# HGRN output norm of a hybrid decoder layer: sums in full fp32 on four groups of 32 partitions, roots on 256 columns, repeated by way of memory

## The chip, the cores and the metric

The kernel runs on one core of one Trainium2 chip. Five engines work beside each other, each through its own queue, in order: TensorE (PE, matrix products and transposes through the array), VectorE (DVE), ScalarE (ACT), GpSimd (POOL), and SyncE (SP), whose queue issues nearly all transfers (DMA) between memory (DRAM) and the on-chip memory of 128 partitions (SBUF). PE writes its products into PSUM, a small memory of banks of 128 x 512 fp32 values. The metric is the device time of one execution in microseconds (us).

## The reference

One inference step of one decoder layer for a prompt of 1024 tokens and eight single new tokens, 1032 columns together. A combined input projection feeds two mixers: a gated linear recurrence (HGRN2, 8 heads of width 128) and a Mamba-2 mixer. Both end in a gated RMS norm, an output projection and a residual; a gated MLP with a convolution follows. The change touches the norm of the HGRN outputs:

```python
def rmsnorm(x, w):
    xf = x.astype(jnp.float32)
    y = xf * lax.rsqrt(jnp.mean(xf * xf, axis=-1, keepdims=True) + EPS)
    return (y * w.astype(jnp.float32)).astype(x.dtype)
...
o_a, S_h_new = hgrn2_mix(heads(q), heads(k), heads(i_r.astype(f32)), heads(log_f), S_h.astype(f32))
o_a = rmsnorm(o_a, w['hgrn_norm_w']) * jax.nn.silu(heads(g_r).astype(f32))
...
x = x + jnp.concatenate([o_a, y], axis=-1) @ w['w_out']
```

For each head and each token the mean runs over the 128 values of the head's output.

## The kernel before

All activations lie transposed: features on the 128 partitions, tokens along the columns. The mean over a head's 128 features is therefore a sum over partitions, and PE takes it: a product with a matrix of ones leaves the same sum in every output partition.

**The driving stream.** The weight products are cut into jobs (one job for each 128 columns of the input projection and for each pair of 128-column blocks of the output projection). A projection job (`in_job`, L290) has three column chunks of 344 tokens; each weight and each activation is split into a high and a low fp32r part, so that one chunk takes 24 products. `drive` (L266) advances the jobs by so many single products for each weight that a second stream yields, and that stream puts its own instructions in between. `tick` (L233) counts the single products, and `after(n, work)` (L229) lets `work` emit its instructions n products later. PE's queue has exactly this order (the block at L1114); on the other engines a planner orders the instructions. `fetch` (L172) is a transfer on SP's queue that is placed behind the last weight load in the queue (`last_w`).

**A head.** `head` (L830) is the second stream for one head: it transposes v, multiplies the decays into k and q in seven levels (`scale`, L867: DVE), forms the products near the diagonal into 32 partitions at a time (`near`, L882), handles the eight single tokens ("od", L939 to L942: eight products into four groups of 32 partitions), builds the states, then the outputs in two halves of 512 tokens. While head h runs, the jobs of head h + 1 drive; while the last head (7) runs, the first output jobs do, from o8.0 on, with the Mamba-2 rows of the mixed activations read and split on the way (`mix_load`, L1021: "ml" and "mh").

**The norm of a head** (L977 to L1008). For each half, ACT squares the outputs twice from PSUM, once rounded to fp32r (`hl`, name "sqhl") and once in fp32 (`sq`); DVE multiplies weight and gate into the output (`oh`, a half of tile `sg`) and forms the low part of the square by a subtraction. One yield of 3.5 later PE sums high and low part with the fp32r ones (`ones_r`, L529) into a bank "hms" of its own per half, 512 columns each. `rstd_of` (L648) makes the reciprocal root: one table function on ACT, then three DVE instructions that refine it. POOL multiplies it into the output (L1003), and SP stores the finished head (`mix_d`, L1008). The eight single tokens have a small norm of their own ("od", "dms"), which the change leaves as it is.

The weight of a projection job is loaded (`ws`, L189), cast by ACT (`wh`, L190), and its low part is taken by DVE (`wl`, L192). Names from the next head's start that the prediction uses: `vd` (L843, L844: a small tile stored to memory and fetched back repeated on all partitions as `vb`, L852), `v<-q,f` (L902), `tt` (L879), `xtd` and `odr` (L798, L944), `xs` (L784, L794).

Of the kernel before, what the change touches and what calls it, by code (L numbers as in the profile page):

```python
# [8 lines left out]
F32 = mybir.dt.float32  # L9
F32R = mybir.dt.float32r  # L10
U8 = mybir.dt.uint8
AF = mybir.ActivationFunctionType
ALU = mybir.AluOpType
# [3 lines left out]
P = 128  # L17
# [3 lines left out]
NT = T + ND  # L21
# [3 lines left out]
H = 8  # L25
# [25 lines left out]
def hybrid_layer(  # L51
# [9 lines left out]
    V, A, G, PE, SP = nc.vector, nc.scalar, nc.gpsimd, nc.tensor, nc.sync  # L61
# [5 lines left out]
    dram = ctx.enter_context(tc.tile_pool(name="dscr", bufs=1, space=DRAM))  # L67
# [3 lines left out]
    def nm(s):  # L71
        cnt[0] += 1
        return f"{s}_{cnt[0]}"
# [4 lines left out]
    const = part.enter_context(tc.tile_pool(name="const", bufs=1, side="right"))  # L78
# [3 lines left out]
    def tl(tag, name, dt=F32):  # L82
        w, n = TAGS[tag]
        return (work if tag in ("hT", "big", "e", "g") else tmp).tile([P, w], dt, tag=tag, bufs=n, name=nm(name))

    def half(name):
        return tl("s", name)[:, :512]

    def bank(s, tag="mx"):
        return psmx.tile([P, 512], F32, tag=tag, bufs=NBANK[tag], name=nm(s))  # L90

    def mm(out, lhsT, rhs, start=True, stop=True):
        PE.matmul(out, lhsT, rhs, start=start, stop=stop)  # L93
# [55 lines left out]
    def col(name, i=0):  # L149
        c = vlay[name] + i  # L150
        return vcol[:, c:c + 1]
# [20 lines left out]
    def fetch(dst, src):  # L172

        with tc.issue_after(last_w[0].ins):
            SP.dma_start(dst, src)
# [53 lines left out]
    def after(n, work):  # L229

        later.append([n, work])
# [109 lines left out]
    mix_d = dram.tile([16, P, NT], F32, name="mix_d")  # L341
# [60 lines left out]
    ones = keep.tile([P, P], F32, name="ones")  # L402
# [24 lines left out]
    for c, cs in enumerate(chunks):  # L427
        ps = psmm.tile([P, 512], F32, tag="mm", name=nm("dt"))
# [96 lines left out]
    for g in range(4):  # L525
        rows = slice(32 * g, 32 * g + 32)
        V.tensor_copy(mlow[rows], lowf[rows, :, rows])
        V.tensor_copy(eyec[rows], ident[rows, rows])
    ones_r = const.tile([P, P], F32R, name="ones_r")  # L529
    V.tensor_copy(ones_r, ones)  # L530

    def ssd_front(g, c, parts):
        tsl = slice(c * P, (c + 1) * P)
# [114 lines left out]
    def rstd_of(dst, tmp, ps, n):  # L648

        A.activation(dst, ps, AF.Abs_reciprocal_sqrt, bias=epsc, scale=1.0 / n)  # L650
        V.scalar_tensor_tensor(tmp, ps, n * EPS, dst, op0=ALU.add, op1=ALU.mult)
        V.scalar_tensor_tensor(tmp, tmp, -0.5 / n, dst, op0=ALU.mult, op1=ALU.mult)
        V.scalar_tensor_tensor(dst, tmp, 1.5, dst, op0=ALU.add, op1=ALU.mult)
# [76 lines left out]
    def once(work):  # L730
        def run():
# [19 lines left out]
    G.affine_select(eye8, eye8, pattern=[[1, ND], [-1, ND]], compare_op=ALU.is_equal, fill=0.0, base=0,  # L751
                    channel_multiplier=0)
    vd_d = dram.tile([H, ND, P], F32, name="vd_d")

    am = const.tile([P, NC, P], F32, name="am")
    G.memset(am, 0.0)
# [73 lines left out]
    def head(h, t):  # L830
        f, k, q, v, sg = (t[n] for n in ("f", "k", "q", "v", "sg"))
# [5 lines left out]
        for hf in range(2):  # L837
            ps = bank("vtp")
# [22 lines left out]
        hb = [slice(0, 512), slice(512, T)]  # L861
        kt, SS, sq = ([None, None] for _ in range(3))
# [57 lines left out]
        ps = bank("a3")  # L920
# [9 lines left out]
        ps, p6 = bank("a5"), bank("a6")  # L930
# [9 lines left out]
        for b in range(ND):  # L940
            g = b % 4
# [5 lines left out]
        for hf in range(2):  # L947
            kt[hf] = half("kt")
            ps = bank("ktp")
# [5 lines left out]
        for hf in range(2):  # L955
            SS[hf] = half("SS")
            ps = bank("kv")
# [16 lines left out]
        yield 3.2  # L974


        hls = []  # L977
        for hf in range(2):
            oh = sg[:, hb[hf]]
            ps = bank("o")  # L980
            for i in range(4):
                n = hf * 4 + i
                Sb, c = before[n], slice(n * P, (n + 1) * P)
                mm(ps[:, blk[i]], vt[hf][:, blk[i]], am[:, n, :], stop=Sb is None)
                if Sb is not None:
                    mm(ps[:, blk[i]], Sb, q[:, c], start=False)
            sq[hf] = half("sq")
            hl = tl("e", "sqhl", F32R)
            A.activation(hl[:, :512], ps, AF.Square)
            A.activation(sq[hf], ps, AF.Square)  # L990
            V.scalar_tensor_tensor(oh, ps, col("hn"), oh, op0=ALU.mult, op1=ALU.mult)
            V.tensor_tensor(hl[:, 512:1024], sq[hf], hl[:, :512].bitcast(F32), op=ALU.subtract)
            hls.append((oh, hl))
        dps = bank("dms", "nx")
        mm(dps[:, :ND], ones, od[:, 1, :])
        rstd_of(od[:, 1, :], od[:, 2, :], dps[:, :ND], P)
        yield 3.5
        for hf, (oh, hl) in enumerate(hls):
            ps = bank("hms")
            mm(ps, ones_r, hl[:, :512], stop=False)  # L1000
            mm(ps, ones_r, hl[:, 512:1024], start=False)
            rstd_of(sq[hf], half("nt"), ps, P)
            G.tensor_tensor(oh, oh, sq[hf], op=ALU.mult)  # L1003

        oh = sg[:, T:NT]
        V.scalar_tensor_tensor(oh, od[:, 0, :], col("hn"), oh, op0=ALU.mult, op1=ALU.mult)
        V.tensor_tensor(oh, oh, od[:, 1, :], op=ALU.mult)
        SP.dma_start(mix_d[h], sg[:, :NT])  # L1008


    def split(src, hi, lo):
# [102 lines left out]
    with tc.manual_schedule(engines={mybir.EngineType.PE}):  # L1114
        finish("x3")
        drive(ssd(0), 45.5, "x7")
        drive(ssd(1), 45.5, "v0")
        finish("z7")
        for h in range(H):
            drive(head(h, heads[h]), 32.0 if h else 35.0, f"sg{h + 1}" if h < H - 1 else "o12.2")  # L1120
        finish("o12.6")
        for r0 in (0, 4):
            mixes[r0] = mix_load(r0)
# [238 lines left out]
    with tc.manual_schedule(engines={mybir.EngineType.PE}):  # L1362
# [43 lines left out]
        def down(w, kt, msl, acts, c):  # L1406
            q = quarters[c]
            ps = psmm.tile([P, 512], F32, tag="mm", name=nm("dn"))[:, :q.stop - q.start]
            for k in range(kt):
                hi, lo = acts[k]  # L1410
                wh, wl = w(k)
                mm(ps, wh[:, msl], hi[:, q], start=(k == 0), stop=False)
                mm(ps, wh[:, msl], lo[:, q], start=False, stop=False)
                mm(ps, wl[:, msl], hi[:, q], start=False, stop=(k == kt - 1))
                tick()
            return ps

        acts = [act_load(k) for k in range(RND)]
        for r0 in range(0, FT - RND, RND):
# [3 lines left out]
            for m in range(0, KT, 2):  # L1423
                wh, wl = wload(w_down[0, rows, m * P:(m + 2) * P], nk, 2 * P)
                for i in range(2):
# [3 lines left out]
                    for c, cs in enumerate(quarters):  # L1429
                        ps = down(lambda k: (wh[:, k, :], wl[:, k, :]), nk, slice(i * P, (i + 1) * P), acts, c)  # L1430
# [14 lines left out]
    for c in (3, 0, 1, 2):  # L1445
        cs = quarters[c]
        for m in range(KT):
            ps = down(lambda k: wd[k], nk, slice(m * P, (m + 1) * P), acts, c)
# [52 lines left out]
```

## Time and profile before

| | us |
|---|---|
| median of 3 runs | 1769.57 (1768.42 to 1771.63) |
| the profiled execution | 1770.87 |
| its span in the trace | 1769.2 |
| TensorE clock granted, mean | 0.993 of full speed |
| norm of the first head: its first sum on PE | 445.2 |
| norm of the last head: its first sum on PE | 884.0 |
| last read of a head's output from memory (`ml`) issued | 954.0 |

A row of grouped instructions reads: line, engine, operation, written tile <- read tiles, shape, count | busy time in us, mean duration of one in ns | idle time of the engine just before. A row of the timeline begins with its start and its duration in us; "x4" means that four such instructions in a row are merged; the bracket names idle time before and what ended it. "SPq" is SP's queue of transfers: the time is that of the issue. A row of waits reads: engine, tile, line <- what ended the wait: us in total, times, longest. A row of windows gives from:to in us, its length, the busy time (and instructions) of PE, PE's weight loads, DVE, ACT and POOL, the granted TensorE clock, the share of the DMA engines, and GB/s. An fp32 product leaves two records on PE, an fp32r product one.

### The profile page before, as it was taken

What the parts mean: (1) busy time and instruction counts of PE and PEld (TensorE: products, weight loads), DVE (VectorE), ACT (ScalarE), POOL (GpSimd) and SP (SyncE); (2) the same over time, 40 slices, a digit from 0 to 9 for tenths busy, and PEclk for the clock granted to TensorE, in tenths of its full rate; (3) what the DMA queues carried; (4) which work ended last, traced back from release to release, by engine and by line L of the source; (5) the groups of instructions that cost most, each with busy time, mean ns of one, the idle gap of its engine ahead of it and who ended that gap; (6) DMA issues with size and microseconds to landing.
All of it is one profiled execution on the core that took longest, in us unless ns stands there. A gap on an engine that the chain in (4) does not pass through costs nothing. (4 is left out here: it accounts for less than half of the span.)

```text
span 1769.2 us, 38520 instructions
## 1 busy us (share of the span) xinstructions
PE 1717.5 (97%) x16079; PEld 1669.4 (94%) x16079; DVE 1123.7 (64%) x2013; ACT 824.7 (47%) x1474; POOL 503.6 (28%) x501
## 2 busy tenths in 40 slices
PE   7999899999999999999899989999999999999998
PEld 6998799989999999999799989999999999999997
DVE  6668967575554565467646677776666667445545
ACT  7577698454545454454423364343333444111114
POOL 2103332120110110112230355766666664000002
PEclk9999999999999999999999999999999999999999
DMA  5355744543221222234336742222222225422212
GB/s 165 66 148 151 188 115 140 179 138 104 76 76 52 85 75 66 71 102 127 113 100 212 244 127 72 72 75 82 96 73 73 73 84 212 151 85 82 97 61 97
DMA packets 247461, 194.95 MB, mean 110 GB/s; under 512 B 46924, under 2 KB 220502, under 8 KB 247270
## 3 DMA queue, kind: packets, MB, share of 16 engines
q1 hardware_dynamic: 246998, 192.38, 36.0%
q8 instruction: 126, 2.06, 0.5%
q14 instruction: 49, 0.40, 0.1%
q0 software_dynamic: 288, 0.10, 0.0%
HBM read 149.92 MB, written 46.91 MB: 111 GB/s over the span
## 5 line engine op out<-in xcount | busy, mean ns | idle before, releaser
L93 PE MATMUL mm<-hh,wh 128*128 128x344 f32 x1248 | 405.7, 326 | 1.6 <-ACT sz L672 1.5
L93 PE MATMUL mm<-hl,wh 128*128 128x344 f32 x1248 | 405.0, 325 | 0.6 <-issue 0.6
L93 PE MATMUL mm<-hh,wl 128*128 128x344 f32 x1248 | 402.2, 323 | 0.0
L93 PEld LDWEIGHTS mm<-hh,wh 128*128 128x128 f32 x1248 | 235.1, 189 | 5.7 <-issue 2.4
L93 PEld LDWEIGHTS mm<-hl,wh 128*128 128x128 f32 x1248 | 235.5, 189 | 3.2 <-issue 1.7
L93 PEld LDWEIGHTS mm<-hh,wl 128*128 128x128 f32 x1248 | 235.6, 189 | 2.1 <-issue 1.4
L190 ACT CAST wh<-ws 128x1024 fp32r<-128x1024 f32 x96 | 100.5, 1047 | 242.5 <-PE dn L93 135.6
L93 PE MATMUL ub<-uh,wh 128*128 128x258 f32 x704 | 199.6, 284 | 0.8 <-DVE fext L1314 0.5
L93 PE MATMUL ub<-ul,wh 128*128 128x258 f32 x704 | 199.3, 283 | 0.0
L93 PE MATMUL ub<-uh,wl 128*128 128x258 f32 x704 | 199.0, 283 | 0.0
L93 PE MATMUL dn<-ah,wh 128*128 128x256 f32 (+1 forms) x640 | 181.2, 283 | 2.0 <-DVE x L1431 2.0
L93 PE MATMUL dn<-al,wh 128*128 128x256 f32 (+1 forms) x640 | 180.5, 282 | 0.0
L93 PE MATMUL dn<-ah,wl 128*128 128x256 f32 (+1 forms) x640 | 180.1, 281 | 0.0
L192 DVE TENSOR_TENSOR wl<-ws,wh 128x1024 fp32r<-128x1024 f32 x88 | 115.0, 1307 | 73.7 <-ACT wh L190 66.9
L93 PE MATMUL mm<-mh,wh 128*128 128x258 f32 x512 | 148.5, 290 | 4.7 <-DVE x L1061 2.9
L93 PE MATMUL ua<-uh,wh 128*128 128x258 f32 x528 | 150.0, 284 | 3.0 <-DVE x L1061 1.8
L93 PE MATMUL ua<-ul,wh 128*128 128x258 f32 x528 | 149.7, 284 | 0.0
L93 PE MATMUL ua<-uh,wl 128*128 128x258 f32 x528 | 148.8, 282 | 0.0
L93 PE MATMUL mm<-ml,wh 128*128 128x258 f32 x512 | 146.7, 286 | 1.7 <-DVE ml L1019 1.7
L93 PE MATMUL mm<-mh,wl 128*128 128x258 f32 x512 | 146.4, 286 | 0.0
L1264 DVE TENSOR_TENSOR wl<-wt,wh 128x512 fp32r<-128x512 f32 x88 | 90.8, 1051 | 75.4 <-ACT wh L1263 75.4
L93 PEld LDWEIGHTS ub<-uh,wh 128*128 128x128 f32 x704 | 133.3, 189 | 1.3 <-DVE fext L1314 0.7
(354 smaller groups left out, 4095.0 us busy)
## 6 DMA issues: line engine op xcount, KB each, us to landing
ws<-in_w_in_dram SPq DMA_DIRECT2D x52, 512.0 KB
ws<-in_w_up_dram SPq DMA_DIRECT2D x44, 512.0 KB
ws<-in_w_out_dram SPq DMA_DIRECT2D x24, 512.0 KB
act_d<-val SPq DMA_DIRECT2D x22, 516.0 KB
al<-act_d SPq DMA_DIRECT2D x22, 516.0 KB
ws<-in_w_down_dram SPq DMA_DIRECT2D x22, 512.0 KB
ml<-mix_d SPq DMA_DIRECT2D x48, 172.0 KB
csb<-cs_d SPq DMA_DIRECT2D x32, 256.0 KB
```

What stands on the lines that cost most here:

```text
L93: PE.matmul(out, lhsT, rhs, start=start, stop=stop)
L190: A.copy(wh[:, :n], ws[:, :n])
L192: V.tensor_tensor(wl[:, :n], ws[:, :n], wh[:, :n].bitcast(F32), op=ALU.subtract)
L1264: V.tensor_tensor(lo[:, cs], sums[name], hi[:, cs].bitcast(F32), op=ALU.subtract)
```

## The change

The squares are taken once, in fp32, and the subtraction and the fp32r ones go. The sums are four fp32 products: group g of 32 output partitions gets the sums of tokens 256 g to 256 g + 255, so that one bank of 256 columns holds all 1024. The roots are made once, on 256 columns, with each value standing 32 times over. One row of each group is stored to memory (`hr_d`, 4 x 256 values); 16 ticks later two transfers bring it back as 512 columns on all 128 partitions, one for each half, into the tiles of the squares; 48 ticks after the sums DVE multiplies them into the output, in place of POOL, and the head is stored.

```diff
-    ones_r = const.tile([P, P], F32R, name="ones_r")
-    V.tensor_copy(ones_r, ones)
...
+    hr_d = dram.tile([H, 4, 256], F32, name="hr_d")
...
-        hls = []
         for hf in range(2):
             oh = sg[:, hb[hf]]
             ps = bank("o")
...
             sq[hf] = half("sq")
-            hl = tl("e", "sqhl", F32R)
-            A.activation(hl[:, :512], ps, AF.Square)
             A.activation(sq[hf], ps, AF.Square)
             V.scalar_tensor_tensor(oh, ps, col("hn"), oh, op0=ALU.mult, op1=ALU.mult)
-            V.tensor_tensor(hl[:, 512:1024], sq[hf], hl[:, :512].bitcast(F32), op=ALU.subtract)
-            hls.append((oh, hl))
         dps = bank("dms", "nx")
         mm(dps[:, :ND], ones, od[:, 1, :])
         rstd_of(od[:, 1, :], od[:, 2, :], dps[:, :ND], P)
         yield 3.5
-        for hf, (oh, hl) in enumerate(hls):
-            ps = bank("hms")
-            mm(ps, ones_r, hl[:, :512], stop=False)
-            mm(ps, ones_r, hl[:, 512:1024], start=False)
-            rstd_of(sq[hf], half("nt"), ps, P)
-            G.tensor_tensor(oh, oh, sq[hf], op=ALU.mult)
+        ps = bank("hms")
+        for g in range(4):
+            mm(ps[32 * g:32 * g + 32, :256], ones[:, 0:32], sq[g // 2][:, g % 2 * 256:g % 2 * 256 + 256])
+        nt = half("nt")
+        rstd_of(nt[:, 0:256], nt[:, 256:512], ps[:, :256], P)
+        SP.dma_start(hr_d[h], nt[::32, 0:256])
 
         oh = sg[:, T:NT]
         V.scalar_tensor_tensor(oh, od[:, 0, :], col("hn"), oh, op0=ALU.mult, op1=ALU.mult)
         V.tensor_tensor(oh, oh, od[:, 1, :], op=ALU.mult)
-        SP.dma_start(mix_d[h], sg[:, :NT])
+
+        def spread_rstd():
+            for hf in range(2):
+                fetch(sq[hf], hr_d[h, 2 * hf:2 * hf + 2].rearrange("a t -> (a t)").unsqueeze(0).to_broadcast([P, 512]))
+
+        def scale_out():
+            for hf in range(2):
+                V.tensor_tensor(sg[:, hb[hf]], sg[:, hb[hf]], sq[hf], op=ALU.mult)
+            SP.dma_start(mix_d[h], sg[:, :NT])
+
+        after(16, spread_rstd)
+        after(48, scale_out)
```

## The prediction

> **What bounds the kernel now.** I read the page first: the engines' line, then the windows of the stretch in which the norms of the eight heads lie (the first at 445 us, the last at 884 us).
>
> ```profile
> span 1769.2 us, 38520 instructions
> PE 1717.5 (97%) x16079; PEld 1669.4 (94%) x16079; DVE 1123.7 (64%) x2013; ACT 824.7 (47%) x1474; POOL 503.6 (28%) x501
> ...
> 445.00:820.00 375.00, 373.83 (x4905) 361.89 (x4904) 207.17 (x388) 185.72 (x299) 48.75 (x36) 1.00 0.27 79
> 820.00:890.00 70.00, 59.96 (x837) 56.98 (x836) 56.04 (x99) 30.90 (x65) 24.64 (x20) 0.93 0.36 108
> ```
>
> TensorE (PE) is busy 97% of the span. From head 1 to head 6 (445 to 820) it has next to no idle time, 373.8 of 375.0, with VectorE (DVE) at some 55%. There only what PE itself does counts. From 820 to 890, where head 7 runs beside the first output products, it differs: DVE 56.04 of 70.00, PE only 59.96, and a granted clock of 0.93. Next, the waits of PE from 780 to 900 us.
>
> ```profile
> PE xtd L798 <- DVE odr L944: 4.2, 1, 4.2
> PE mm L93 <- DVE ml L1019: 1.7, 1, 1.7
> PE a L93 <- DVE v L874: 1.3, 1, 1.3
> ...
> 832.00:835.00 3.00, 3.00 (x16) 2.75 (x15) 2.93 (x8) 2.04 (x5) 0.17 (x1) 0.53 0.99 300
> 860.00:866.00 6.00, 5.97 (x28) 5.94 (x29) 0.88 (x2) 0.57 (x2) 0.00 (x0) 0.50 0.06 19
> ```
>
> DVE ends 4.2 + 1.7 + 1.3 = 7.2 us of these waits. After the second largest and the largest of them the granted clock drops to about half. So two places can move the time: PE's cost of the norm's sums, eight times, and DVE's load around the start of head 7.
>
> **The sums on PE.** Removed per head: four fp32r products of 512 columns. Added: four fp32 products of 256 columns, each into 32 partitions. For the old price I take the order in time at head 0; for the new one no row exists, and the nearest is "od", eight fp32 products of 128 columns into the same four groups of 32 partitions (sixteen records, since an fp32 product leaves two), beside "n2ms", fp32 on the full width with 258 columns.
>
> ```profile
> 445.18 1.08 PE L93 MATMUL hms<-sqhl,ones_r 128*128 128x512 f32 x4
> 446.10 0.32 PE L93 MATMUL mm<-hh,wh 128*128 128x344 f32 x1
> ...
> 546.34 0.64 PE L93 MATMUL od<-Sh,qb 128*32 128x128 f32 x16
> 546.91 0.43 PE L93 MATMUL mm<-hh,wh 128*128 128x344 f32 x1
> 547.18 0.32 PE L93 MATMUL mm<-hl,wh 128*128 128x344 f32 x1
> 547.34 0.32 PE L93 MATMUL mm<-hh,wl 128*128 128x344 f32 x1
> ...
> 519.71 0.32 PE L93 MATMUL mm<-hh,wh 128*128 128x344 f32 x1
> 519.96 0.73 PE L93 MATMUL a<-q,k 128*32 128x32 f32 x62
> ...
> L93 PE MATMUL hms<-sqhl,ones_r 128*128 128x512 f32 x32 | 8.7, 394 | 0.0
> L93 PE MATMUL od<-Sh,qb 128*32 128x128 f32 x128 | 5.2, 279 | 0.0
> L93 PE MATMUL n2ms<-n2r,ones 128*128 128x258 f32 x8 | 2.2, 380 | 0.0
> ```
>
> Old: 446.10 - 445.18 = 0.92 us per head. New: od streams 16 x 128 = 2048 columns, as the new sums will (8 records x 256). It starts at 546.34 and releases PE at 546.91: 0.57 us. Two changes of shape come with it: a product follows its forerunner here by 0.16 us (547.18 to 547.34), the narrow ones start 0.25 us after the last wide one (519.71 to 519.96), and the first wide one after od keeps PE for 0.27 (546.91 to 547.18), so 0.09 + 0.11 = 0.20. New price 0.77 us, a gain of 0.15 per head and 1.2 us in eight. The other end: were the four groups not to run side by side, each record would cost what n2ms shows, 2.2 / 8 = 0.275 us; 8 of them and 0.20 make 2.4, a loss of 1.48 per head and 11.8 us. I take the od end, because od has the same height of 128 partitions, the same groups, the same order of pairs, and shows 5.2 / 128 = 41 ns per record where a 128-column fp32 record with nothing beside it would need some half of n2ms's 275. The removed copy of the ones (one DVE instruction) and the table loads of ScalarE (ACT), which stay, count nothing: DVE is idle near half the time there.
>
> A rule that speaks against this: the Trainium skill, page "FP8 and Floating Point Precision", counts a true fp32 product as four passes through the array. By it alone, on the skill's 2.4 GHz ("TensorE: Matmul & The Clock Gate"), the new sums would be 4 x 4 x 256 columns, estimated 1.7 us against 0.85 before: 8 x 0.85 = 6.8 us slower. od's row shows that four groups together take about a quarter of that, so the row decides.
>
> **ACT, DVE and GpSimd (POOL) around it.** Per head ACT loses two squares and its two roots on 512 columns, and gains one on 256; DVE loses two subtractions and six root steps on 512 columns, gains three on 256 and the two final products; POOL loses its two products.
>
> ```profile
> L992 DVE TENSOR_TENSOR sqhl<-sq,sqhl 128x512 fp32r<-128x512 f32 x16 | 10.9, 681 | 0.0
> L651 DVE SCALAR_TENSOR_TENSOR nt<-n2ms,n2r x4: 417/423/427, 996.6 to 1065.9; 128x258 f32<-128x258 f32 x4
> ...
> 511.11 1.29 DVE L651 SCALAR_TENSOR_TENSOR nt<-hms,sq 128x512 f32<-128x512 f32 x2 [5.09 <-ACT sq L650]
> 513.52 1.29 DVE L653 SCALAR_TENSOR_TENSOR sq<-nt,sq 128x512 f32<-128x512 f32 x2
> 515.97 2.30 DVE L192 TENSOR_TENSOR wl<-ws,wh 128x1024 fp32r<-128x1024 f32 x1 [0.53 <-ACT wh L190]
> 518.20 1.21 DVE L902 TENSOR_TENSOR v<-q,f 128x1024 f32<-128x1024 f32 x1
> 519.47 0.68 DVE L879 TENSOR_TENSOR tt<-f 128x512 f32<-128x512 f32 x1
> ...
> 524.74 1.78 DVE L874 TENSOR_TENSOR q<-v,tt 128x512 f32<-128x512 f32 x1
> ...
> 528.50 0.75 PE L93 MATMUL a<-q,f 128*32 128x32 f32 x64
> ```
>
> A root step on 258 columns has a row (423 ns), so three take 1.27 us in place of 514.81 - 511.11 = 3.70. The final products are DVE products of two 512-column operands in SBUF, like the subtraction: 2 x 0.68 = 1.36. In heads 1 to 6 PE hides all this. What is late next there is the column of DVE work that ends with q at 526.52, which PE needs at 528.50: 1.98 us of cover.
>
> **The way through memory.** New on SP's queue per head: one small store, two fetches of 256 KB repeated to 128 partitions, and the store of the head's output, which moves back behind the final product. The trace has a twin: vd stored, then fetched repeated.
>
> ```profile
> 500.66 0.56 SPq L175 DMA_DIRECT2D rt<-in_state_conv_ffn_dram  x1
> 515.47 0.29 SPq L844 DMA_DIRECT2D vd_d<-vd  x1
> ...
> 518.13 1.24 SPq L175 DMA_DIRECT2D vb<-vd_d  x2
> ...
> 523.14 1.13 POOL L853 TENSOR_TENSOR vb<-vb,k 128x512 f32<-128x512 f32 x1 [5.95 <-DMA vb<-vd_d]
> ...
> 457.38 0.81 SPq L175 DMA_DIRECT2D vb<-vd_d  x2
> 461.09 1.37 POOL L853 TENSOR_TENSOR vb<-vb,k 128x512 f32<-128x512 f32 x1 [7.11 <-DMA vb<-vd_d]
> ```
>
> From the store's issue to the fetch's is 518.13 - 515.47 = 2.66 us, from there to the first user 5.01, and 3.71 at the head before (457.38 to 461.09): 6.4 to 7.7 in all. In head 1 the new root steps start no later than the old (511.11), so the store goes out near 511.1 + 1.3 = 512.4, the fetches near 515.1, and the data is there between 518.8 and 520.1. The final product is released 48 ticks behind the sums; a tick is one product of the driving stream, 0.16 us, so that is some 7.7 us, or near 517. On DVE it comes about with v at 518.20 (which may move forward itself, since the wl split of 2.30 us then runs without POOL's products beside it; I don't count on it). Behind the waiting product on DVE stand the tt products and the scalings that end with q. Early end: it is over at 518.8 + 1.4 = 520.2, 0.7 us behind the old start of tt (519.47); late end: 521.5, 2.0 behind. Against 1.98 of cover the early one costs nothing, and the late one just uses it up. On SP the waiting fetch stops only what is behind it, and the row at 500.66 is the last issue ahead of 515.47; the output's store moves past vd, vb and one weight load, and in the code its data is read only behind job o12.6, six output jobs later at the soonest: nothing.
>
> **The start of head 7.** Here DVE sets the end. These are its rows.
>
> ```profile
> 816.41 1.01 DVE L1019 TENSOR_TENSOR ml<-ml,mh 128x344 fp32r<-128x344 f32 x2 [1.09 <-ACT mh L1018]
> 817.49 1.29 DVE L651 SCALAR_TENSOR_TENSOR nt<-hms,sq 128x512 f32<-128x512 f32 x2
> ...
> 821.10 3.98 DVE L1019 TENSOR_TENSOR ml<-ml,mh 128x344 fp32r<-128x344 f32 x4
> 820.73 3.12 POOL L1003 TENSOR_TENSOR sg<-sg,sq 128x512 f32<-128x512 f32 x2 [45.30 <-ACT mh L1018]
> 826.05 1.21 DVE L902 TENSOR_TENSOR v<-q,f 128x1024 f32<-128x1024 f32 x1
> ```
>
> Root steps: 3.7 less 1.27 = 2.4 gained. The four splits at 821.10 take 3.98 us while POOL's products run; undisturbed they cost 0.5 each (1.01 for the two at 816.41), 2.0: 1.9 gained. Final product: 1.36 lost, and it can wait: with the root steps from 817.49 the store goes out near 818.8 and the data lands between 825.2 and 826.5, while v, 4.3 us earlier, would start near 822 and end near 823. Further splits and the small products fill most of the gap, so I take 0.5 lost (0 to 2.5). Balance 2.4 + 1.9 - 1.4 - 0.5 = 2.4 us sooner; as PE waits 7.2 us for DVE behind this point, all of it arrives. The bounds: 0.4 the wrong way, if the whole landing is waited out, and 7.2 the right way, if each wait goes.
>
> **The sum.** -1.2 (PE) - 2.4 (head 7) = -3.6 us on the profiled 1770.87 (span 1769.2 and 1.7 around it): 1767.3. The median shown is 1.3 below that run, so **1766.0**, its own range 1763.5 to 1768.5.
>
> **Rivals.**
>
> 1. *The slow clock after 860 goes too.* The row from 860 to 866 shows 6 us at 0.50, so 3.0 us are lost there. If the wait of 4.2 us shrinks to 1.8, this may not happen: 1763.0. Against it: the drop at 832 followed a wait of only 1.7 us, so a short one suffices here. The Trainium skill, "TensorE: Matmul & The Clock Gate", Part 1, says that the clock halves after at least one idle window of about 3.4 us; by that rule the drop would vanish. The trace speaks against so firm a bound, hence 0.13.
>
> 2. *Head 7's gain is eaten.* The final product waits on DVE in the one stretch where DVE is last, and gives the 2.4 back: -1.2 remains, 1768.4. For it: the splits' own fetches crowd the queues there. 0.16.
>
> 3. *The product stalls DVE in every head* (the other side). Place: DVE's queue ahead of tt. It decides when the data lands past the late end above, about 520.1 in head 1's times. Each further microsecond goes straight to PE in seven heads: +7, less 1.2 and with no gain in head 7, +5.8 for one microsecond: 1775.4. For it: at the late end no margin is left. Against it: nothing is queued ahead of the fetches on SP from 500.66 to 515.47. 0.16.
>
> 4. *The groups run one after another.* +11.8 - 2.4 = +9.4: 1779.0. od speaks against it. 0.10.
>
> **How the numbers follow.** A measurement of this kernel tells 0.2%, 3.5 us, from no change. The forecast has 0.45; its 3.6 us lie on that bound, and as its sure parts point down I put 0.29 of it under faster and 0.16 under same. Faster: 0.29 + 0.13 = 0.42. Same: 0.16 + 0.16 = 0.32. Slower: 0.16 + 0.10 = 0.26. The range runs from 1760.5, case 1 with 2.5 us more of the waits, to 1778, 1.4 us of stall per head in case 3 (7 x 1.4 - 1.2 = +8.6); it leaves out most of case 4 and the tails.
>
> **What would show it.** The sums: 8 records per head on PE, first to the next wide product 0.57 us (right) or over 2 (case 4). DVE's three root steps at 0.42 each, no POOL product in the heads' norm, splits at 821 at 0.5 each. The final product: DVE's idle time ahead of it, ended by the DMA; under 1 us is right, 3 or more with a PE wait on q (L874) behind it is case 3. In 820 to 870, the wait of xtd for odr at 2 us or less, and the clock at 862. The forecast is wrong if PE's idle time between 445 and 820 grows by more than 2 us.

## The result, and the profile after

The kernel after takes 1764.49 us (median of 14 runs, 1761.33 to 1769.15) against 1769.59 for the kernel before beside it (14 runs): a ratio of 0.9973, 95% interval 0.9965 to 0.998. That is 4.8 us less (3.5 to 6.2); forecast were 3.6 and 1766.0. The profiled execution took 1763.89 us, its span is 1762.2.

The page after (engines' line), and the windows of the same two stretches:

```profile
PE 1713.2 (97%) x16111; PEld 1662.8 (94%) x16111; DVE 1105.4 (63%) x1988; ACT 812.3 (46%) x1450; POOL 482.0 (27%) x485
...
445.00:820.00 375.00, 373.80 (x4941) 359.53 (x4940) 196.39 (x375) 176.10 (x282) 33.00 (x24) 1.00 0.30 88
820.00:890.00 70.00, 60.19 (x853) 57.58 (x851) 49.55 (x92) 26.41 (x57) 18.82 (x16) 0.93 0.41 125
```

PE's busy time fell by 4.3 us, from 1717.5 to 1713.2. That isn't the sums alone: a product at half clock is busy for longer (0.42 us for 0.28 around 833 us in the kernel before), so the stretches of slow clock below are part of it. From 445 to 820 PE is as full as before (373.80 of 375), though DVE has 11 us less work, ACT 10 and POOL 16, so nearly all that these three lost was hidden there. One wait of the kernel before was not. In head 1 PE stood half a microsecond for the small norm of the single tokens (od):

```profile
PE cst L333 <- DVE od L651: 0.5, 1, 0.5
```

The list of PE's waits from 445 to 820 has this row in every run in which head 1 has the old norm (before, e1, e3, e9, e12), and in none of the others. What the kernel after has there instead is a single gap of 1.2 us for which the profile names no releaser. Its second execution (e4, below) has no gap at all and is busy for 374.97 us.

**The sums**, in head 1, PE in order of time:

```profile
505.96 0.32 PE L93 MATMUL mm<-hh,wh 128*128 128x344 f32 x1
506.21 0.64 PE L93 MATMUL hms<-sq,ones 128*32 128x256 f32 x8
506.78 0.43 PE L93 MATMUL mm<-hl,wh 128*128 128x344 f32 x1
507.04 0.32 PE L93 MATMUL mm<-hh,wl 128*128 128x344 f32 x1
```

From the first sum to the next wide product 506.78 - 506.21 = 0.57 us. The sums start 0.25 us after the last wide product instead of 0.16, and that next product holds PE for 0.26 instead of 0.16: 0.09 + 0.57 + 0.10 = 0.76 in all, where 0.77 was forecast.

**The way through memory** in head 1; DVE in order of time, from the first root step to q:

```profile
507.45 0.42 DVE L649 SCALAR_TENSOR_TENSOR nt<-hms,nt 128x256 f32<-128x256 f32 x1 [3.72 <-ACT nt L648]
...
513.52 1.23 DVE L192 TENSOR_TENSOR wl<-ws,wh 128x1024 fp32r<-128x1024 f32 x1 [0.53 <-ACT wh L190]
514.66 1.22 DVE L901 TENSOR_TENSOR v<-q,f 128x1024 f32<-128x1024 f32 x1
...
515.93 1.28 DVE L1009 TENSOR_TENSOR sg<-sg,sq 128x512 f32<-128x512 f32 x2
...
521.97 1.78 DVE L873 TENSOR_TENSOR q<-v,tt 128x512 f32<-128x512 f32 x1
```

SP's queue there, the store of the roots (hr_d) and their two fetches (sq):

```profile
508.82 0.52 SPq L997 DMA_DIRECT2D hr_d<-nt  x1
510.56 0.82 SPq L175 DMA_DIRECT2D sq<-hr_d  x2
```

A root step takes 0.42 us. The product at 515.93 has no idle time in front, 7.1 us behind the store's issue, and q ends at 523.75 (before: 526.52). The wl split takes 1.23 us in place of 2.30: POOL's product no longer works beside it (in e9, the kernel before with only that product moved to DVE, the split takes 1.21). In DVE's waits from 380 to 960 the repeated roots appear once:

```profile
DVE sg L1009 <- DMA sq<-hr_d: 0.7, 1, 0.7
```

**The start of head 7**, DVE's splits, v and the final product in order of time:

```profile
816.14 1.79 DVE L1024 TENSOR_TENSOR ml<-ml,mh 128x344 fp32r<-128x344 f32 x4
...
820.37 1.23 DVE L901 TENSOR_TENSOR v<-q,f 128x1024 f32<-128x1024 f32 x1 [0.60 <-PE vtp L839]
821.51 0.68 DVE L1009 TENSOR_TENSOR sg<-sg,sq 128x512 f32<-128x512 f32 x1
```

PE's waits from 780 to 900:

```profile
PE mm L93 <- ACT x L1064: 2.8, 1, 2.8
PE xtd L797 <- DVE odr L943: 2.6, 1, 2.6
...
PE mm L93 <- DVE ml L1024: 0.8, 1, 0.8
```

The same wait for ACT in the kernel before:

```profile
PE mm L93 <- ACT x L1059: 1.6, 2, 1.1
```

Windows of the kernel after: behind its wait for ml (ended at 825.0), behind its wait for x (ended at 839.0) and a gap of 1.9 us for which the profile names no releaser (ended at 843.6), and behind its wait for odr:

```profile
825.00:829.00 4.00, 3.98 (x31) 3.83 (x32) 4.00 (x7) 2.23 (x5) 2.79 (x3) 1.00 0.61 189
844.00:848.00 4.00, 4.00 (x22) 4.00 (x22) 4.00 (x8) 2.36 (x6) 0.00 (x0) 0.57 0.95 275
855.00:861.00 6.00, 5.71 (x26) 5.69 (x27) 1.00 (x4) 0.38 (x1) 0.00 (x0) 0.50 0.12 43
```

Four splits take 1.79 us (before 3.98); v starts at 820.37 instead of 826.05, 3.0 of it because the whole head begins sooner (its first transpose at 819.3 instead of 822.3); neither final product waits. The wait for ml shrank from 1.7 to 0.8 us, and no slow clock follows it. But the slow clock that stood at 832 to 835 (0.53) isn't gone: one of the same size comes some ten microseconds later, 844 to 848 at 0.57, which costs 4 x 0.43 = 1.7 us. The second execution (e4) has it from 839 to 843. The wait for odr (4.2 us before) is 2.6 and still followed by half a clock, 855 to 861. That it shrank doesn't hold up: e4, the same kernel, shows 4.2 again, and e1, the kernel before, 4.5. The wait for ACT's copy x is 2.8 and 2.0 us in the two executions of the kernel after, 1.6 and 1.9 in those of the kernel before.

### The profile page after: what moved, and what is told of

Same layout as the page of the kernel before. It is cut to its first block, busy times and chain, and to the rows that moved or that the text cites. A ratio compares the mean times of both kernels' runs of the same rounds, so it can differ in the third digit from the quotient of the medians.

```text
span 1762.2 us, 38558 instructions
## 1 busy us (share of the span) xinstructions
PE 1713.2 (97%) x16111; PEld 1662.8 (94%) x16111; DVE 1105.4 (63%) x1988; ACT 812.3 (46%) x1450; POOL 482.0 (27%) x485
## 5 line engine op out<-in xcount | busy, mean ns | idle before, releaser
L192 DVE TENSOR_TENSOR wl<-ws,wh 128x1024 fp32r<-128x1024 f32 x88 | 108.7, 1235 | 75.7 <-ACT wh L190 68.6
```

The source lines that it names most:

```text
L192: V.tensor_tensor(wl[:, :n], ws[:, :n], wh[:, :n].bitcast(F32), op=ALU.subtract)
```

## The experiments

The first table reads all traces in one way: how much longer or shorter than in the first trace of before each stretch of PE's queue took. Its marks are the first transpose of v in head 0 (383.4 us in that trace) and in head 7 (822.3), the first residual transpose xtd (834.2), the first sum of the second norm (995.5) and the first product of the last stage, fin (1735.1). One row is one execution; the ratio is from the timed runs, each kernel against the kernel before, timed beside it.

| kernel | heads 0-6 | head 7 begins | to second norm | rest | ratio, interval |
|---|---|---|---|---|---|
| after | -0.95 | -2.85 | +1.86 | -2.74 | 0.9973, 0.9965 to 0.998 |
| e4 after again | -2.96 | -2.88 | +0.86 | -1.56 | 0.9968, 0.9956 to 0.9981 |
| e1 before again | -1.07 | -0.08 | +0.05 | -0.13 | 1.0003, 0.9992 to 1.0013 |
| e2 new norm in heads 0-5 | -1.39 | -1.20 | -1.74 | -0.36 | 0.9986, 0.9976 to 0.9997 |
| e3 new norm in heads 6, 7 | +0.05 | -2.38 | +0.33 | -1.33 | 0.9988, 0.9978 to 0.9998 |
| e5 sums twice | +0.31 | -2.43 | -0.01 | -0.99 | 0.9996, 0.9987 to 1.0005 |
| e6 late fetch | -2.58 | -2.87 | +3.19 | -0.39 | 0.998, 0.9969 to 0.9992 |
| e7 product on POOL | +5.74 | -1.22 | -2.27 | -0.60 | 1.0013, 1.0003 to 1.0024 |
| e8 sums beside narrow ones | +9.12 | -0.83 | +1.20 | +1.00 | 1.0044, 1.003 to 1.0058 |
| e9 DVE product only | +0.66 | -3.72 | +5.59 | +0.41 | 0.9997, 0.9988 to 1.0005 |
| e10 full-width sums | +4.58 | -3.72 | +2.02 | -0.44 | 1.0009, 1.0 to 1.0017 |
| e11 after, vb by POOL | -2.78 | -2.87 | +1.62 | +1.07 | 0.9968, 0.9956 to 0.9981 |
| e12 e9, vb by POOL | +1.89 | -3.74 | +6.59 | -1.97 | 1.0014, 1.0001 to 1.0026 |

e1 shows how far a row can be trusted: the same kernel differs by 1.07 us in the heads. Ahead of the first mark, where next to nothing is changed, the rows lie between -2.07 (after) and +2.77 (e12). Three rows have the norm of the kernel after in all places up to head 7 (after, e4, e11), and their heads span 2 us. In the last stage lies work that no edit touches, yet it runs from -2.74 to +1.07. A single row tells differences of some 2 us; the start of head 7 is steadier, within 0.03 us for these three. There, with the product on DVE, all rows lie between -2.38 and -3.74 (e8, whose product comes later, apart), with POOL's between 0 and -1.22.

The -1.20 of e2 needs a word, since its heads 6 and 7 have the old norm. PE's wait for ml there and the clock behind it:

```profile
PE mm L93 <- DVE ml L1045: 1.7, 1, 1.7
827.00:832.00 5.00, 3.83 (x30) 3.67 (x30) 4.93 (x10) 2.17 (x5) 1.63 (x3) 1.00 0.79 242
```

The wait is as long as in the kernel before, but no slow clock follows, and there that cost 1.0 us up to the mark. So about 1 us of such a row can be the clock alone.

**e1 and e4: both kernels again, unchanged.**

> The kernel before, unchanged, with a profile of its own. Theory (two places: the sums on PE, and DVE at the start of head 7): the order of every engine is the same as in the changed kernel up to the first head's norm and again in the MLP, so what the two traces differ by there (2.1 us by 383 us, 2.7 us between 1000 and 1075 us) is chance of one execution, and this second trace of the same kernel will differ from the first one by 1 to 3 us in those same stretches. Rival (the change acts there too, by where its work ends): this trace lies within 0.5 us of the first one in both stretches. Ratio to before 1.000.

> The changed kernel, unchanged, with a second profile and more times. Both theories: ratio 0.997. Theory: its offset to the first trace of the changed kernel varies by 1 to 3 us in the stretches before 383 us and from 1000 to 1075 us, while the sums on PE again take 0.57 us from the first to the next wide product in each head. Rival: within 0.5 us of the first trace there.

Measured 1769.5 and 1764.22 us. The difference stands. Of the scatter expected, the two traces of the kernel after show 3.0 us by the first mark, those of the kernel before only 0.5; around the second norm the latter differ by 1.7 us, which is one stretch of slow clock (see the end of the next section).

**e2 and e3: the new norm in some heads only**, the rest with the old one.

```diff
+    NEW = range(6)          # e3: (6, 7)
...
+            if h not in NEW:
+                V.tensor_tensor(hl[:, 512:1024], sq[hf], hl[:, :512].bitcast(F32), op=ALU.subtract)
...
+        if h in NEW:
+            ps = bank("hms")
```

> The new norm in heads 0 to 5 only, the old one in heads 6 and 7. Theory: only the sums count there, 6 x 0.15 = 0.9 us faster than before (ratio 0.9995); head 7's start as in the kernel before, with the splits near 820 us at about 1 us each. Rival (the gain comes from less work on DVE, ACT and POOL everywhere): 6/8 of 4.8, 3.6 us faster (0.998).

> The new norm in heads 6 and 7 only. Theory: 0.3 us by the sums and 1.3 to 2.4 us at the start of head 7, where DVE sets the end: 1.6 to 2.7 us faster than before (0.9985 to 0.999). Rival (less work everywhere): 2/8 of 4.8, 1.2 us faster.

Measured 1766.69 and 1767.42 us, 0.14% and 0.12% below before; together 0.26%; the whole change gave 0.27 and, in e4, 0.32%. So the gain has two parts of like size, one in the heads and one around head 7. The intervals, 0.1% either way, don't settle the size of each better than by 2 us: for e2 both the 0.9 us expected and the rival's 3.6 lie inside.

**e5: the four sums made twice.**

```diff
-        for g in range(4):
+        for g in (0, 1, 2, 3, 0, 1, 2, 3):
```

> Against the changed kernel: each head's four sums are made twice into the same bank, eight more records per head. Theory (the four groups run side by side and PE's time is the kernel's time there): 0.45 to 0.57 us more per head without a further change of shape, 3.6 to 4.6 us in all; ratio to before about 0.9995. Rival (the groups one after another): 8 x 2.2 = 17.6 us more. Second rival (PE's time in the heads is hidden by something else): no change against the changed kernel.

Measured 1767.93 us, by the ratios 4.1 above the kernel after (0.9996 less 0.9973 of 1769.6). PE in head 1, in order of time:

```profile
507.48 1.07 PE L93 MATMUL hms<-sq,ones 128*32 128x256 f32 x16
508.48 0.43 PE L93 MATMUL mm<-hl,wh 128*128 128x344 f32 x1
```

From the first sum to the next wide product 1.00 us, where one set takes 0.57: four more sums cost 0.43 us, 8 x 0.43 = 3.4 in eight heads. So nothing hides a sum on PE, and of the 0.57 only 0.43 is streaming. The four groups must overlap for that: at the pace of the wide fp32r products, 344 columns in 0.16 us, eight records of 256 columns one behind another would take 0.95 us.

**e10: the sums on the full width**, with roots on 512 columns and no way through memory.

```diff
-        ps = bank("hms")
-        for g in range(4):
-            mm(ps[32 * g:32 * g + 32, :256], ones[:, 0:32], sq[g // 2][:, g % 2 * 256:g % 2 * 256 + 256])
...
+        for hf in range(2):
+            ps = bank("hms")
+            mm(ps, ones, sq[hf])
+            rstd_of(sq[hf], half("nt"), ps, P)
...
-        after(16, spread_rstd)
```

> The kernel after with one edit: the sums are made on the full width of 128 output partitions, two fp32 products of 512 columns into a bank each, with roots on 512 columns for each half; so nothing goes by way of memory, and DVE multiplies the roots in directly, 48 ticks behind the sums as before. What PE streams is the same 2048 record columns as in the kernel after (4 records of 512), but nothing runs side by side. Theory (four groups of 32 partitions run beside each other, at about a quarter of the price): a full-width fp32 record costs what n2ms shows, 0.275 us for 258 columns, so 4 of 512 cost 2.2 us against 0.57 plus 0.20 for the groups: +1.4 us for each head and +11.4 in eight, and head 7 loses 2.4 of its gain on the root steps: 1774 to 1779 us, 10 to 15 over the kernel after. Rival (the groups are no faster than the full width, and 0.57 us is what 2048 columns cost in any form): within 1 us in the heads, 1764 to 1767. On PE the first sum to the next wide product shows it directly: 2.2 us or 0.6.

Measured 1771.43 us, by the ratios 6.4 to 7.3 above the kernel after and e4, between theory and rival. PE at head 0, in order of time:

```profile
444.58 1.88 PE L93 MATMUL hms<-sq,ones 128*128 128x512 f32 x4
445.89 0.72 PE L93 MATMUL mm<-hh,wh 128*128 128x344 f32 x1
446.46 0.32 PE L93 MATMUL mm<-hl,wh 128*128 128x344 f32 x1
```

The next wide product starts 1.31 us behind the first sum and then holds PE for 0.57 instead of 0.16, so 1.31 + 0.41 = 1.72 us for the same 2048 columns of records that the four groups stream in 0.43: four times as much. The groups do run side by side. Against 0.76 this is 0.96 per head and 7.7 in eight, near what the timed runs show; the 2.2 expected was too high. So was the expectation that head 7 loses 2.4 us to the larger root steps: its start gained 3.72. The Trainium skill, "FP8 and Floating Point Precision", TensorE Precision Notes, counts a true fp32 product as four passes; at the skill's 2.4 GHz ("TensorE: Matmul & The Clock Gate") that is an estimated 4 x 1024 columns or 1.71 us here, and the trace agrees with 1.72.

**e6: the fetches 44 ticks behind the sums instead of 16.**

```diff
-        after(16, spread_rstd)
+        after(44, spread_rstd)
```

> Against the changed kernel: the two fetches are released at 44 ticks in place of 16, 28 x 0.157 = 4.4 us later; the final product keeps its place on DVE. Theory of the prediction's third rival, priced: in head 1 the product stood at 515.93 us without a wait and the fetches left at 510.56; they will leave near 515 and land 3.7 to 5 us later, so DVE waits 3 to 4 us ahead of the product, uses up some 2.4 us of cover in front of q, and PE waits 0.5 to 1.5 us per head for q: 4 to 10 us slower than the changed kernel. Other view (the cover is larger): DVE waits, PE does not, no change.

Measured 1765.69 us, 0.998 (0.9969 to 0.9992): not told apart from e4. SP's queue in head 1, the store of the roots and their two fetches:

```profile
510.01 0.53 SPq L997 DMA_DIRECT2D hr_d<-nt  x1
511.75 0.35 SPq L175 DMA_DIRECT2D sq<-hr_d  x1
...
514.61 0.34 SPq L175 DMA_DIRECT2D sq<-hr_d  x1
```

DVE's second final product:

```profile
518.01 0.69 DVE L1009 TENSOR_TENSOR sg<-sg,sq 128x512 f32<-128x512 f32 x1 [0.20 <-DMA sq<-hr_d]
```

The window of heads 1 to 6:

```profile
445.00:820.00 375.00, 374.97 (x4955) 360.66 (x4948) 197.51 (x376) 177.13 (x284) 33.08 (x24) 1.00 0.30 89
```

The edit did less than it was to do: the first fetch still goes out 1.74 us behind the store (in the kernel after 510.56 - 508.82, the same), only the second is later, by some 2.4 us. It is issued at 514.61, the product that needs it starts 3.4 us later, and DVE waits 0.20 us. PE loses nothing from 445 to 820. The 4 to 10 us expected did not come. So this much lateness stays inside the cover; more was not tried.

**e7: the final product back on POOL**, everything else as after.

```diff
-                V.tensor_tensor(sg[:, hb[hf]], sg[:, hb[hf]], sq[hf], op=ALU.mult)
+                G.tensor_tensor(sg[:, hb[hf]], sg[:, hb[hf]], sq[hf], op=ALU.mult)
```

> Against the changed kernel: the final product goes back to POOL, all else stays. Theory: in heads 1 to 6 nothing; at the start of head 7 DVE saves 1.36 us and loses about as much, since the splits that run beside POOL's product take twice their time: within 1 us of the changed kernel. Rival (moving the product to DVE is what made the gain): 2 us or more slower than the changed kernel.

Measured 1771.91 us: slower than before, and 7 above the kernel after. The theory fell. POOL's final products in head 1, here and then in the kernel before:

```profile
515.09 3.94 POOL L1009 TENSOR_TENSOR sg<-sg,sq 128x512 f32<-128x512 f32 x2 [49.87 <-DMA sq<-hr_d]
```

```profile
514.34 2.85 POOL L1003 TENSOR_TENSOR sg<-sg,sq 128x512 f32<-128x512 f32 x2 [48.15 <-ACT sg L819]
```

DVE in the kernel of e7 beside them, v, tt and q:

```profile
515.57 2.31 DVE L901 TENSOR_TENSOR v<-q,f 128x1024 f32<-128x1024 f32 x1
...
517.93 1.65 DVE L878 TENSOR_TENSOR tt<-f 128x512 f32<-128x512 f32 x1
...
527.08 0.69 DVE L873 TENSOR_TENSOR q<-v,tt 128x512 f32<-128x512 f32 x1
```

The largest of PE's waits from 445 to 820:

```profile
PE a L93 <- DVE q L873: 2.6, 2, 1.3
```

The window of that stretch:

```profile
445.00:820.00 375.00, 368.44 (x4893) 354.15 (x4892) 202.99 (x352) 169.81 (x270) 57.17 (x36) 1.00 0.28 84
```

POOL's two products, 3.94 us, now lie beside v and the first tt. v takes 2.31 us (1.22 in the kernel after), tt 1.65 (0.69), six smaller tt's behind them 4.29 (2.40) beside POOL's work on vb, and q ends at 527.77 instead of 523.75 (0.9 of it because this head began later). PE waits, and is busy for 368.44 us instead of 373.80. In the kernel before the same products ran earlier and beside the wl split (2.30 us at 515.97), and q was still in time. So it isn't only which engine makes the product: with the roots late, the DVE instructions that it meets are those PE waits for. The Trainium skill, "SBUF — State Buffer", section on the two separate sides, has a rule for this: a VectorE instruction with two SBUF inputs and a GpSimd one that reads SBUF take one shared port pair in turn, and the loser waits for the whole instruction. The doubled durations agree.

At the start of head 7 e7 gained 1.22 us, but not by shorter waits. PE waits longer for ml than in the kernel before (2.4 for 1.7), and no slow clock follows:

```profile
PE mm L93 <- DVE ml L1024: 2.4, 1, 2.4
833.00:838.00 5.00, 4.19 (x33) 4.04 (x34) 5.00 (x10) 1.39 (x3) 2.20 (x2) 1.00 0.69 246
```

**e8: sums, roots and product moved behind the next head's first narrow products**, to save the change of shape.

```diff
+    pending = []
...
+        if pending:
+            pending.pop()()
...
+        def norm():
+            ps = bank("hms")
...
+        if h < H - 1:
+            pending.append(norm)
+        else:
+            norm()
```

> Against the changed kernel: in heads 0 to 6 the four sums wait on PE until the next head's first narrow products (near, groups of 32 partitions too), so that one change of shape per head goes. Theory (0.20 us per head are the two changes between wide and narrow): 7 x 0.20 = 1.4 us faster in the sums, if the later roots and product find their cover on DVE; head 7's start can lose up to 2 us, since roots and product move into its loaded stretch. Rival (the 0.20 belongs to the fp32 products themselves): no gain in the sums.

Measured 1777.16 us, 13 above the kernel after. PE at the first sums, in order of time:

```profile
456.25 0.64 PE L93 MATMUL hms<-sq,ones 128*32 128x256 f32 x8
456.70 0.80 PE L93 MATMUL a<-q,k 128*32 128x32 f32 x64
```

DVE's waits from 445 to 820:

```profile
DVE sg L1015 <- DMA sq<-hr_d: 25.6, 9, 5.5
```

PE's waits there:

```profile
PE a L93 <- DVE q L874: 4.2, 7, 2.0
```

The sums did get cheaper: 0.45 us to the next narrow product, which leaves the change of shape for the rest of the 0.76. But now the product stands in DVE's loaded column and waits for its data, up to 5.5 us and 25.6 in all, with the scalings behind it; PE waits 4.2 us for q and 2.9 for v. This is rival 3 of the prediction, the product that stalls DVE ahead of tt and q, brought about by this edit.

**e9: the kernel before with the final product on DVE**, and nothing else.

```diff
-            G.tensor_tensor(oh, oh, sq[hf], op=ALU.mult)
+            V.tensor_tensor(oh, oh, sq[hf], op=ALU.mult)
```

> The kernel before with one edit: DVE makes the final product instead of POOL; squares, sums and 512-column roots stay, nothing goes by way of memory. Theory (the sums' price and the smaller root steps and POOL's absence beside the splits are separate gains): nothing changes on PE in heads 0 to 6 (first sum of head 0 to first sum of head 6: the time of before within 0.5 us). At the start of head 7 the four splits that took 3.98 us beside POOL take 2.0, the two products cost DVE 1.36, the root steps stay at 3.70: about 0.5 us sooner in all, so 0 to 1.5 us under the kernel before, ratio 0.9990 to 1.0005. Rival 1 (what head 7 gained was POOL's absence alone): the whole 1.3 to 2.4 us of head 7 come with this edit, and the later stretch behind them: 3 to 5 us under before, ratio 0.9970 to 0.9985. Rival 2 (the products on DVE cost more than POOL's collisions): slower than before by 1 us or more.

Measured 1769.58 us: no difference, as the theory said, but for another reason. At the start of head 7 this one edit gained 3.72 us, more than the whole change (2.85). Then all was lost again, in a profiled execution of 1773.35 us, 3.8 above this kernel's median, so the loss is shown here at its larger end. The largest of PE's waits from 780 to 900:

```profile
PE mm L93 <- ACT x L1059: 7.3, 2, 6.1
```

ACT's cast of ml in order of time:

```profile
837.30 0.48 ACT L1018 CAST mh<-ml 128x344 fp32r<-128x344 f32 x1 [3.83 <-DMA ml<-mix_d]
```

POOL's residual additions:

```profile
828.26 5.88 POOL L791 TENSOR_TENSOR x<-x,xs 128x512 f32<-128x512 f32 x3 [53.29 <-DVE ml L1019]
```

SP's queue, the ml fetches behind the fetch of vb (issued at 832.73):

```profile
833.10 0.91 SPq L175 DMA_DIRECT2D ml<-mix_d  x2
```

and what vb waited for there, in SP's waits from 822 to 845:

```profile
SPq L175 <- POOL x L791: 3.4, 1, 3.4
```

POOL's three residual additions took 5.88 us beside DVE's scalings; SP's fetch of vb waited 3.4 us for them; the ml fetches behind it went out at 833.10; ACT's cast mh waited 3.83 us for them, the copy x behind it on ACT came late, and PE stood for 7.3 us.

**e11 and e12: vb of head 7 fetched by POOL's queue**, in the kernel after and in e9's.

```diff
-            fetch(vb, vd_d[h, bs].rearrange("b n -> (b n)").unsqueeze(0).to_broadcast([P, 512]))
+            vsrc = vd_d[h, bs].rearrange("b n -> (b n)").unsqueeze(0).to_broadcast([P, 512])
+            if h == H - 1:
+                G.dma_start(vb, vsrc)
+            else:
+                fetch(vb, vsrc)
```

> The kernel after with one edit: in the last head (7) the two repeated fetches of vb are issued by POOL's queue instead of SP's. Theory: in the kernel after SP's queue stands 5.0 us (two waits, longest 3.1) for POOL's residual additions (x) ahead of the fetch of vb at 828.11, and three fetches of ml stand behind it, at 828.48; their late data stops ScalarE's copies (3.69 us ahead of mh at 832.50), and the copy x behind them stops PE for 2.8 us. With vb on POOL's own queue the ml fetches go out about 3 us sooner, right behind the weight load at 824.57, and that wait of PE goes: 2 to 3 us sooner by the transpose xtd that stands at 860.0 in the kernel before, 1760 to 1763 in all. Rival 1 (the ml fetches are held by PE's products that free their tiles as well, 0.3 us of it shown; or vb is what is late next): within 1 us of the kernel after, 1763.5 to 1765.5. Rival 2 (transfers issued by POOL cost its additions and DVE time): slower than the kernel after by 1 us or more.

> The kernel of e9 (before, with the final product on DVE) with the same edit: vb of head 7 by POOL's queue. In e9 PE was 3.7 us sooner at the first transpose xtd of head 7 (834) and had lost all of it by 860: SP's fetch of vb stood 3.4 us for POOL's x additions, the ml fetches behind it went out at 833.10, ACT's mh waited 3.83 us for them, and PE 6.1 us for ACT's x. Theory (the SP queue behind vb is what took head 7's gain back): the wait of 6.1 us goes or is 2 at most, and most of the 4 us stays: 1765 to 1767.5. Rival (POOL's x additions themselves, 1.96 us each beside DVE there, or the split ladder behind them, set the end): the wait only changes its name, 1768.5 to 1770.

Measured 1765.12 and 1771.91 us: no gain in the first, and the second slower than before. The theory fell in both. SP's waits from 815 to 862 in e12:

```profile
SPq L860 <- POOL Sh L859: 12.2, 2, 10.3
```

(This execution, 1776.41 us, was the slowest of its eleven.) SP no longer waits ahead of vb, but 12.2 us ahead of the two stores of Sh, which wait for POOL's sum with vb, and the ml fetches stand behind that instead. PE's wait for x is 9.4 us. The next instruction in the queue that depends on POOL took over the wait. That the ring of POOL, SP's queue, ml, ACT and PE gives the gain back is read from the rows; which link would have to be shortened isn't settled by these runs.

## Why the prediction held, step by step

**The sums: right.** Forecast were 0.57 and 0.77 us; the rows show 0.57 and 0.76. The saving of 0.15 per head is too small for the stage table to confirm. The heads gave a little more than the sums: the wait of 0.5 us for od in head 1, which the prediction put at nothing, went too. The row taken for the price (od) was the right one, for the reason given: e10 shows that without groups the same columns take 1.72 us. The other end of the range, 2.4 (2.2 for the records and 0.20 for the shape), was mis-sized: it took the mean busy time of n2ms's records, 0.275 us for 258 columns, where e10 has 1.72 / 4 = 0.43 for 512, half of it for 256. By e10, rival 4 would stand 1.72 + 0.20 - 0.77 = 1.15 us per head above the forecast, 9.2 us in eight, where the text has 13 (from -3.6 to +9.4). The rule of four passes in the Trainium skill ("FP8 and Floating Point Precision", TensorE Precision Notes), decided against there, holds for the full width; here four groups pass at once.

**The way through memory: right.** Landing and cover held, with 0.7 us of DVE's waits in all. e6 shows that 2.4 us of lateness of one fetch are still free, e8 what the landing costs where there is no cover. That the wl split would lose its collision (1.23 for 2.30) was seen and not booked.

**The start of head 7: size near, working wrong.** Forecast -2.4, measured -2.85 to -2.88 in three executions, up to the first xtd. But the terms don't add as the text had them. Root steps were to bring 2.4 of it; e9 and e10 keep them at 512 columns and gain 3.7. e7 has the small root steps, and its 1.2 is the slow clock that didn't come, as in e2, which has the old ones. What counts is that POOL's product leaves, and then the gain ends where PE has nothing more to win. The window of the kernel before from head 7's first transpose to the first xtd shows how much that is:

```profile
822.00:834.20 12.20, 9.84 (x189) 9.07 (x187) 12.16 (x19) 5.32 (x12) 4.30 (x4) 0.92 0.37 120
```

PE is idle for 12.20 - 9.84 = 2.36 us, 1.7 of them the wait for ml, and loses 0.08 x 12.2 = 1.0 to the slow clock that follows: 3.4 us, of the 3.72 that e9 gained (0.3 isn't accounted for). The 0.8 us that the kernel after still waits for ml are about what it lacks against e9.

The step that failed is "as PE waits 7.2 us for DVE behind this point, all of it arrives". The rows of PE's waits from 780 to 900 add up to 9.9 us in both executions of the kernel before, and to 9.8 and 10.8 in those of the kernel after: when DVE is ready sooner, PE waits as long, only further on, for ACT's x and again for odr (2.6 and 4.2). And the slow clock moved instead of going. So the stretch to the second norm gives 0.86 to 1.86 us back, and head 7 as a whole brings 1.0 to 2.0 us, not 2.4. That the row of the first stretch came out near the forecast is luck: 1.0 us of it is the slow clock at 832, which the sum did not have and which comes back behind the mark.

**Rival 1** (the slow clock after 860 goes) did not come: half a clock from 855 to 861, behind a wait of 2.6 us; the sign named for it, a wait for odr of 2 us or less, failed too. **Rival 2** came in another form: the final product waited for nothing, but a third to two thirds of the first stretch's gain were given back behind it. **Rival 3** is the one that e8 shows to be real, and this kernel stays clear of it: its product comes 7.1 us behind the store.

**Not in the sum at all:** 2.74 us behind the second norm in the profiled execution. No instruction there is changed. Summed over windows of 2 us, PE is idle for 8.7 us there in the first trace of the kernel before and loses 1.7 to a stretch of half clock; in the trace of the kernel after it is 7.6 and nothing. The second trace of the kernel before has no slow clock there either, but 10.1 us of idle time, and e4 and e11, with the new norm, have the slow clock again. So it is scatter of waits and clock. The stretch in question, in the first and the second trace of the kernel before, behind the same wait for x (1.77 and 1.70 us):

```profile
1046.00:1052.00 6.00, 5.24 (x31) 5.25 (x32) 5.97 (x9) 3.78 (x8) 5.93 (x5) 0.72 0.13 44
1045.00:1051.00 6.00, 6.00 (x49) 6.00 (x50) 5.97 (x8) 4.55 (x10) 5.37 (x6) 1.00 0.17 58
```

**What stays open:** sums (1.3 in eight heads), od (0.5) and head 7 (1.0 to 2.0) make 2.8 to 3.8 us, at the lower end of the 3.5 to 6.2 measured. What the rest is, if it is more than scatter, these runs don't show.

No kernel that was run beats the kernel after beyond the intervals.

## What to carry to other kernels

- Where one engine is full, price an edit by that engine's order in time, from the last instruction ahead to when the next runs at its usual pace, not by mean durations: the fp32 sums in four groups were read so to the hundredth, and the bound taken from a mean was off by 0.5 us (2.2 for 1.72).
- An elementwise product on GpSimd isn't free because GpSimd is idle: look at which VectorE instruction it will lie beside, and who waits for that one.
- A gain ahead of a wait is worth at most that wait and what it triggers, and a slow clock that is gone in one place can come back a little later: compare up to a mark well behind it. Behind it the next link of the ring has to be looked at, and moving one transfer to another queue may only change which instruction stands there.

## What the runs showed of the hardware

- Half the clock came after short waits of PE: 1.7 us in the kernel before (0.53 from 832), 2.6 us in the kernel after. It did not come after 1.7 us in e2, 2.4 in e7 and 1.70 in e1, where the same wait of 1.77 in the first trace brought it. So the length of one wait doesn't decide; what does is not shown here. The Trainium skill, "TensorE: Matmul & The Clock Gate", Part 1, gives one idle window of about 3.4 us as the condition; these traces don't agree with it as a condition on one gap.
- Around head 7 such a stretch cost 1.7 us (4 us at 0.57, 844 to 848 in the kernel after) or twice that (859 to 867 at 0.57 in the kernel before, 8 x 0.43 = 3.4).
- Four fp32 products into four groups of 32 output partitions took a quarter of the full-width time, 0.43 against 1.72 us, and the changes of shape around them 0.33 us (0.76 less 0.43).
- VectorE instructions with two SBUF operands took about twice their time beside GpSimd's: v 2.31 for 1.22 (e7 and after), four splits 3.98 for 1.79 (before and after).
